# Reads of the turned queries and keys of the second attention, and its rotary steps: another place in the queue and another engine

## The chip, the cores and the metric

The kernel runs on one core of one Trainium2 chip. The metric is the device time of one execution in microseconds. Five engines work beside each other, each through its own queue of instructions in a fixed order: TensorE (PE) multiplies matrices, with its weight loads counted apart (PEld), VectorE (DVE), ScalarE (ACT) and GpSimd (POOL) work on tiles, and SyncE (SP) issues nearly all DMA transfers. An instruction waits on semaphores for what it reads or overwrites, and whatever stands behind it in its queue waits with it.

## The reference

A decoder trunk of two layers on 256 tokens of width 1024, in float32. In each layer:

```
h = rms_norm(x)
cq, ckv, k_rope, mq, mk, mv, rq, rk, rv, rg, g_mla, g_moba, g_ret = split(h @ w_in)
o_mla  = mla_branch(...)          # first attention: 8 heads, low-rank q and kv, rotary part of 32
o_moba = moba_branch(mq, mk, mv)  # second attention: 8 heads of 64, rotary on the first 16 of 64
o_ret  = retention_branch(...)    # 4 heads, rotary on all 64, chunks of 128, group norm
x = x + (sigmoid(g_mla) * (o_mla @ w_mla) + sigmoid(g_moba) * (o_moba @ w_moba)
         + sigmoid(g_ret) * (o_ret @ w_ret)) @ w_out
x = x + square(relu(rms_norm(x) @ w_up)) @ w_down
```

and a final rms_norm. With 256 tokens and blocks of 256 the second attention is plain causal attention within one block: softmax(q k^T / 8) v, where q and k have had `apply_rope`, [x1 c - x2 s, x1 s + x2 c], on their first 16 columns. c and s are tables of position and frequency.

## The kernel before

Every product is made of three float32r matmuls: weight and activation are split in a high and a low part, and hi*hi, hi*lo, lo*hi are summed (`three`, lines 300 to 303). Weights come in blocks of 128 x 1024 (512 KB) by SyncE's queue (`transfer`, line 213) into one of seven raw buffers; ScalarE copies the high part (line 280), VectorE subtracts for the low part (line 282), six buffers each. `load_w` fetches one block beyond the one in use in the order of the program, but the planner, which orders each engine's queue by a simulated timeline with the program's order as precedence, lets later blocks go ahead as buffers come free.

The program of a layer is a list of units, each some matmuls of one weight block: the compressed queries and keys of the first attention and mq (mixed in layer 0, unit "start"; units "b0" and "mq" in layer 1), mk (4 blocks), then qrope, mv 0, qnope, mv 1, kvup, mv 2, mv 3, then the gates gmla0, gmla1, gmoba0, gmoba1 of four blocks each, then rqk, rv, rg, gret0, gret1, the branches, w_out and the MLP. Other work is hung on units by `at(slot(key, j), step)`: the step is traced right after that unit. The steps around the change are these.

- `qrope` (layer line 951) leaves in `qr` the rotary columns of the first attention's queries; `swapped` (line 509) moves them, with halves exchanged, through four DMAs of SyncE into `qkoth`. `qr_rope`, at mv 0, multiplies both by tables (line 969) and adds them into the tile Q (lines 972 and 973; four adds, of which head h needs one).
- The first attention's scores (`ps_s`, line 995) of heads 0 to 3 stand at mv 3, so ahead of the gates, and those of heads 4 to 7 seven units later. The softmax is on VectorE and ScalarE (lines 556 to 574), the turned probabilities go out and back through DRAM (lines 611 and 619).
- `exchange` takes the projected mq or mk, scales the two row tiles on ScalarE (line 881), turns 32 x 32 blocks on VectorE (line 331), and calls `exchanged`: one write of 512 KB to a DRAM tile `bounce` (line 478), and eight reads of 128 KB from it (line 483), four into a tile in head order and four into a tile with the partner halves (mqraw and mqoth, mkraw and mkoth). It does so for retention's rqk as well.
- `rope_turned` makes one half of the heads: raw times cos, partner times sin (line 499), and the sum of both (line 500) in a tile qkT. For mq and mk, through `moba_rope`, the three run on GpSimd; for retention's rqk on VectorE. In layer 1 moba_rope stands at mv 0, mv 2, gmla0 1 and gmla0 3, in layer 0 at gmla1 1, gmla1 2, gmoba0 0 and gmoba0 1. The tables TAB are loaded once (line 983), traced behind the unit mv 3 of layer 0, which has fetched the block gmla0 0.
- The second attention's scores (line 543) read qkT at gmoba1 1 and, for heads 4 to 7, eight units later.

`tc.keep_in_program_order(i)` puts the instruction i behind the one traced just before it in its engine's queue. It ties i to nothing else: others may pass between, and it doesn't wait for anything to finish.

Of the kernel before, what the change touches and what calls it, by code (L numbers as in the profile page):

```python
# [7 lines left out]
F32 = mybir.dt.float32  # L8
# [6 lines left out]
P = 128  # L15
D = 1024
S = 256
# [134 lines left out]
def trunk(ctx: ExitStack, tc: tile.TileContext, gx, wts, consts, gfin, gn, xtok, out):  # L152


    nc = tc.nc
# [6 lines left out]
    dr = ctx.enter_context(tc.tile_pool(name="dr", bufs=1, space=bass.MemoryType.DRAM))  # L162
# [9 lines left out]
    TAB = cp.tile([P, 2 * S], F32, name="TAB")  # L172
# [23 lines left out]
    behind = {}  # L196
# [97 lines left out]
    def w2k(name):  # L294
        return sb.tile([P, 512], F32, name=name, tag="w2k", bufs=W2K)
# [12 lines left out]
    def halves(tile_):  # L308
        return tile_.rearrange("p (two s) -> p two s", two=2)
# [17 lines left out]
    def blocks_tile(name):  # L327
        return sb.tile([P, 4 * S], F32, name=name + "blocks", tag="probT", bufs=2)

    def turn_row(blocks, t, row):  # L330
        return nc.vector.transpose(blocks.rearrange("p (b j t e) -> p t j b e", b=4, j=4, t=2)[:, t], row)
# [137 lines left out]
                i = turn * count + j  # L469
                prog.append(((key, i), lambda i=i, ts=ts, j=j: unit(i, ts, j)))  # L470

    def exchanged(rows, name, tags):

        blocks = blocks_tile(name)
        for t in range(NT):
            turn_row(blocks, t, rows[t])
        bounce = dr.tile([P, 4 * S], F32, name="bounce", bufs=2)
        nc.sync.dma_start(bounce, blocks)
        both = [wp.tile([P, 4 * S], F32, name=name + part, tag=tag, bufs=1) for part, tag in zip(("raw", "oth"), tags)]
        for flip, dst in enumerate(both):  # L480
            for b in range(4):
                src = bounce.rearrange("(a p) (b r) -> b p a r", a=4, b=4)[b ^ flip]
                nc.sync.dma_start(dst[32 * b : 32 * b + 32, :].rearrange("p (a r) -> p a r", a=4), src)  # L483
        return both

    def rope_turned(both, tab, i, engine, pins=((), ())):

        o = sb.tile([P, 2 * S], F32, name="qkT", bufs=4)
        wide = o.rearrange("p (j t a e) -> p j t a e", j=2, t=NT, a=4)
        raw, other = (w.rearrange("p (a j t e) -> p j t a e", a=4, j=4, t=NT)[:, 2 * i : 2 * i + 2] for w in both)  # L490
        cos, sin = (
            tab[:, S * k : S * k + S].rearrange("p (t a e) -> p t a e", t=NT, a=4)[:, None].to_broadcast([P, 2, NT, 4, 32])
            for k in range(2)
        )
        for on, dst, src, by, after in ((engine, wide, raw, cos, pins[0]), (nc.gpsimd, other, other, sin, pins[1])):
            with ExitStack() as pinned:
                for ins in after:
                    pinned.enter_context(tc.issue_after(ins.ins))
                (engine if engine is nc.vector else on).tensor_mul(dst, src, by)
        engine.tensor_add(wide, wide, other)  # L500
        return halves(o)

    def swapped(raw, late=False):
# [259 lines left out]
    def at(slot, step):  # L763
        steps.setdefault(slot, []).append(step)

    def slot(key, j):
        return [k for k, _ in prog].index((key, j))
# [9 lines left out]
    def layer(l, xn, before):  # L777

        c0 = []
        c, mla, mqkv, rqkv = {}, {}, {}, {}  # L780
# [91 lines left out]
        qkT = {"mq": {}, "mk": {}}  # L872

        def moba_rope(key, i):
            qkT[key][i] = rope_turned(mqkv[key], TAB, i, nc.gpsimd)

        def exchange(key, accs):

            rows = [w2k("rows") for _ in range(NT)]
            for t in range(NT):  # L880
                nc.scalar.activation(rows[t], accs[t], AF.Copy, scale=xn.col[t])
            mqkv[key] = exchanged(rows, key, ("tsums", "thi") if key == "mk" else ("tlo", "exch"))

        if l:
            project(l, "mq", xn, 512, lambda accs: exchange("mq", accs))
            for n in range(KD):
                at(slot("b0", 7), lambda n=n: xn.square(n))
            at(slot("b0", 7), c_copies)
            at(slot("mq", 0), c_squares)
            at(slot("mq", 1), c_norms)  # L890
        else:
            mq = []
            for k in range(KD):
                prog.append((("start", k), lambda k=k: start(k, mq)))
            at(slot("start", KD - 2), lambda: xn.stats_rows(xrows))
            at(slot("start", KD - 1), c_copies)
            at(slot("start", KD - 1), c_squares)
            at(slot("start", KD - 1), c_norms)
            at(slot("start", KD - 1), lambda: exchange("mq", mq))
        project(l, "mk", xn, 512, lambda accs: exchange("mk", accs))  # L900


# [78 lines left out]
        th_mla = gates(l, "gmla", xn)  # L981
        if l == 0:
            at(slot("mv", 3), lambda: tc.keep_in_program_order(nc.sync.dma_start(TAB, consts[:, K_TURNED_MB:])))
        for i in range(2):
            if l:
                at(slot("mv", 2 * i), lambda i=i: moba_rope("mq", i))
                at(slot("gmla0", 1 + 2 * i), lambda i=i: moba_rope("mk", i))
        first = slot("mv", 3)
        at(first, lambda: omlaT.extend((t4("omlah"), t4("omlal"))))

# [25 lines left out]
            tc.keep_in_program_order(nc.sync.dma_start(rqkv["dec"][:, cs], consts[:, K_DEC:K_TURNED_RT]))  # L1016

        merged, mT = {}, []
        if l == 0:

            for i, (key, j) in enumerate((("gmla1", 1), ("gmla1", 2), ("gmoba0", 0), ("gmoba0", 1))):
                at(slot(key, j), lambda i=i: moba_rope(("mk", "mq")[i % 2], i // 2))
        first = slot("gmoba1", 1)
        at(first, lambda: omobaT.extend((t4("omobah"), t4("omobal"))))

# [24 lines left out]
        def ret_exchange(accs):  # L1050
            rows = [w2k("rows") for _ in range(NT)]
            for t in range(NT):
                nc.scalar.activation(rows[t], accs[t], AF.Copy, scale=xn.col[t])
            rqkv["both"] = exchanged(rows, "rqk", ("tsums", "thi"))

        def ret_rope(i):
            tab = rqkv["dec"][:, RT_H * 3 * P :]
            rT.append(rope_turned(rqkv["both"], tab, i, nc.vector, ((), behind["po"][1:] if i else ())))

        rT, or_ps, aT, rg, oret, oret_T = [], [], {}, {}, [], []  # L1060

# [67 lines left out]
        def oret_split():  # L1129
            oretT.extend((t4("oreth"), t4("oretl")))  # L1130
            have(4)
            with tc.issue_after(fetched[-1].ins):
                split_turned(oret_T[0], oretT)

        project(l, "rqk", xn, 512, ret_exchange)
        project(l, "rv", xn, 512, ret_done("rv"))
        for i in range(2):
            at(slot("rv", 2 + i), lambda i=i: ret_rope(i))
# [401 lines left out]
        for t in range(NT):  # L1540
            y = sb.tile([P, D], F32, name="y", tag="t4", bufs=T4)
            r = sb.tile([P, 1], F32, name="fr", tag="st", bufs=SMALL)
# [34 lines left out]
    for l in range(L):  # L1577
        xn, before = layer(l, xn, before)
# [97 lines left out]
```

## Time and profile before

| | |
|---|---|
| Median of 3 runs | 813.29 us (813.04 to 814.06) |
| Profiled execution | 813.15 us, span 811.4 us |
| Granted TensorE clock, mean | 0.995 |
| ScalarE busy | 488.6 us, 744 instructions |
| HBM traffic | 243 GB/s over the span |

The span is the time from the first to the last instruction of the profiled execution; its own time has 1.75 us more around it. "Busy" is the time in which an engine worked on some instruction. A matmul's row shows 0.39 us from issue to end, though one is issued every 0.23 us: they overlap, and their starts are what counts. In a row of waits, the wait is put down to the instruction whose semaphore came last. In a timeline, like instructions in a row are merged (x4), and the second column runs from the first one's start to the last one's end.

### The profile page before, as it was taken

The numbers are of one execution on the slowest core, as the hardware profiler recorded it, in microseconds if no ns is written. First come the engines' busy times: TensorE is split into PE (matmuls) and PEld (weight loads), VectorE is DVE, ScalarE is ACT, GpSimd is POOL, SyncE is SP. The second block draws the span as 40 slices with busy tenths as digits, with TensorE's granted clock in tenths as the row PEclk, the third lists the DMA queues.
The fourth block names the chain that finished last, engine by engine and source line by source line (L and its number), as shares of the span: only waits on it lengthen the run. The fifth ranks groups of instructions, "written<-read, shape, count | busy, mean of one in ns | idle before, by whom it ended". The sixth has DMA issues, their size and how long they took to land.

```text
span 811.4 us, 11168 instructions
## 1 busy us (share of the span) xinstructions
PE 798.2 (98%) x3815; PEld 660.4 (81%) x3815; DVE 663.8 (82%) x1112; ACT 488.6 (60%) x744; POOL 72.0 (9%) x61
## 2 busy tenths in 40 slices
PE   9998999999999999999999999999999999999997
PEld 7886887778888888888898788877888888888885
DVE  6749975988797888888797796679798888899785
ACT  7782755454476566666486756654535666667572
POOL 0136000010030000000014700001000300000000
PEclk9998999999999999999999999999999999999999
DMA  9995997787666777778739759687846677688851
GB/s 333 397 248 182 283 293 249 182 299 226 233 211 215 246 263 260 257 245 255 243 126 298 244 216 323 220 226 242 298 157 246 225 237 284 213 302 301 271 181 53
DMA packets 73880, 198.38 MB, mean 245 GB/s; under 512 B 8416, under 2 KB 31072, under 8 KB 73824
## 3 DMA queue, kind: packets, MB, share of 16 engines
q1 hardware_dynamic: 73248, 196.81, 73.9%
q10 hardware_dynamic: 576, 0.87, 0.3%
q8 instruction: 30, 0.49, 0.2%
q14 instruction: 26, 0.21, 0.1%
HBM read 175.10 MB, written 22.02 MB: 243 GB/s over the span
## 4 chain that ended last, share of the span: by engine, by line
PE 81%; DMA 7%; DVE 5%; ACT 2%; SPq 2%; issue 1%; POOL 0%; DVEq 0%; ACTq 0%
PE acc L301 16%; PE acc L303 15%; PE acc L302 15%; PE pup L301 8%; PE pup L302 8%; PE pup L303 8%; PE acc L1233 6%; DMA raw<-wts 3%; DVE wlo L282 2%; PE ps_s L995 2%; DMA bounce<-rqkblocks 1%; SPq L483 1%; ACT whi L280 1%; DMA rqkoth<-bounce 1%; DMA xrow<-xtok 1%
## 5 line engine op out<-in xcount | busy, mean ns | idle before, releaser
L282 DVE TENSOR_TENSOR wlo<-raw,whi 128x1024 fp32r<-128x1024 f32 (+3 forms) x263 | 311.7, 1202 | 68.8 <-ACT whi L280 66.9
L280 ACT ACTIVATE whi<-raw 128x1024 fp32r<-128x1024 f32 (+3 forms) x263 | 264.4, 1019 | 170.6 <-PE acc L303 95.5
L301 PE MATMUL acc<-whi,xs 128*128 128x512 f32 (+1 forms) x384 | 150.2, 393 | 0.8 <-ACT th L675 0.8
L302 PE MATMUL acc<-wlo,xs 128*128 128x512 f32 (+1 forms) x384 | 150.3, 392 | 0.0
L303 PE MATMUL acc<-whi,xs 128*128 128x512 f32 (+1 forms) x384 | 149.0, 389 | 0.0
L302 PE MATMUL pup<-wlo,xs 128*128 128x512 f32 x256 | 99.8, 390 | 0.0
L303 PE MATMUL pup<-whi,xs 128*128 128x512 f32 x256 | 99.6, 389 | 0.0
L301 PE MATMUL pup<-whi,xs 128*128 128x512 f32 x256 | 99.4, 389 | 0.0
L301 PEld LDWEIGHTS acc<-whi,xs 128*128 128x128 f32 x384 | 72.2, 188 | 16.7 <-ACT th L675 1.3
L303 PEld LDWEIGHTS acc<-whi,xs 128*128 128x128 f32 x384 | 72.3, 188 | 14.4
L302 PEld LDWEIGHTS acc<-wlo,xs 128*128 128x128 f32 x384 | 72.4, 189 | 14.2
L303 PE MATMUL acc<-whi,sq 128*128 128x512 f32 x184 | 71.8, 390 | 0.0
L301 PE MATMUL acc<-whi,sq 128*128 128x512 f32 x184 | 71.8, 390 | 0.0
L302 PE MATMUL acc<-wlo,sq 128*128 128x512 f32 x184 | 71.6, 389 | 0.0
L303 PEld LDWEIGHTS pup<-whi,xs 128*128 128x128 f32 x256 | 48.1, 188 | 10.0
L302 PEld LDWEIGHTS pup<-wlo,xs 128*128 128x128 f32 x256 | 48.1, 188 | 9.8
L301 PEld LDWEIGHTS pup<-whi,xs 128*128 128x128 f32 x256 | 47.9, 188 | 9.7
L565 ACT ACTIVATE prob<-prob,smx 128x128 f32<-128x128 f32 x64 | 28.3, 444 | 42.0 <-DVE smx L562 42.0
L392 POOL TENSOR_TENSOR sqsum<-sqsum,xsq 128x256 f32<-128x256 f32 x16 | 18.3, 1141 | 303.1 <-ACT xs L317 164.8
L303 PEld LDWEIGHTS acc<-whi,sq 128*128 128x128 f32 x184 | 34.5, 188 | 7.8 <-DVE sq L322 0.6
L301 PEld LDWEIGHTS acc<-whi,sq 128*128 128x128 f32 x184 | 34.6, 188 | 7.0
L302 PEld LDWEIGHTS acc<-wlo,sq 128*128 128x128 f32 x184 | 34.5, 188 | 7.1
(274 smaller groups left out, 1265.8 us busy)
## 6 DMA issues: line engine op xcount, KB each, us to landing
raw<-wts SPq DMA_DIRECT2D x264, 512.0 KB, 5.1
bounce<-hblocks SPq DMA_DIRECT2D x16, 512.0 KB, 3.7
hturned<-bounce SPq DMA_DIRECT2D x64, 128.0 KB, 3.1
pbounce<-blocks SPq DMA_DIRECT2D x8, 768.0 KB, 6.2
probT<-pbounce SPq DMA_DIRECT2D x32, 192.0 KB, 5.4
raw<-wts SPq DMA_DIRECT2D x5, 464.0 KB, 6.0
raw<-wts SPq DMA_DIRECT2D x4, 416.0 KB, 4.1
dec<-consts SPq DMA_DIRECT2D x2, 768.0 KB, 8.9
```

The lines of the kernel that those rows point to most:

```text
L280: fetched.append(nc.scalar.activation(hi[:, cs], raw[:, cs], AF.Copy))
L282: nc.vector.tensor_sub(lo[:, cs], raw[:, cs], hi[:, cs].bitcast(F32))
L301: nc.tensor.matmul(o, ah, bh, start=start, stop=False, **more)
L302: nc.tensor.matmul(o, ah, bl, start=False, stop=False, **more)
L303: nc.tensor.matmul(o, al, bh, start=False, stop=stop, **more)
L392: (nc.gpsimd if n < self.on_pool else nc.vector).tensor_add(self.sum, self.sum, sq)
L483: nc.sync.dma_start(dst[32 * b : 32 * b + 32, :].rearrange("p (a r) -> p a r", a=4), src)
L565: nc.scalar.activation(p[:, a:b], p[:, a:b], AF.Exp, bias=m[:, 2 + i : 3 + i], scale=d**-0.5, accum_out=m[:, 4 + i : 5 + i])
L995: nc.tensor.matmul(bank[:, o], mla["Q"][:, h, qs], mla["K"][:, h, ks], start=True, stop=True)
L1233: nc.tensor.matmul(o, a, b, start=half == 0 and i == 0, stop=4 * half + n == KD and i == len(jobs) - 1)
```

## The change

The eight reads of `exchanged` become a function of their own, `partners`, and for mq and mk they are traced at the units gmla0 0 and gmla0 2, each pinned behind the one traced before it on SyncE's queue. The DRAM tile of the write-out gets a name of its own with four slots. `rope_turned` loses its engine: all its steps run on VectorE. `moba_rope` stands at gmla1 1, gmla1 2, gmoba0 1 and gmoba0 3 in both layers, in the order mk, mq, mk, mq. For retention the reads still follow the write at once.

```diff
-    def exchanged(rows, name, tags):
+    def exchanged(rows, name):
 
         blocks = blocks_tile(name)
         for t in range(NT):
             turn_row(blocks, t, rows[t])
-        bounce = dr.tile([P, 4 * S], F32, name="bounce", bufs=2)
+        bounce = dr.tile([P, 4 * S], F32, name="rowsbounce", bufs=4)
         nc.sync.dma_start(bounce, blocks)
+        return bounce
+
+    def partners(bounce, name, tags):
+
         both = [wp.tile([P, 4 * S], F32, name=name + part, tag=tag, bufs=1) for part, tag in zip(("raw", "oth"), tags)]
         for flip, dst in enumerate(both):
             for b in range(4):
                 src = bounce.rearrange("(a p) (b r) -> b p a r", a=4, b=4)[b ^ flip]
-                nc.sync.dma_start(dst[32 * b : 32 * b + 32, :].rearrange("p (a r) -> p a r", a=4), src)
+                dma = nc.sync.dma_start(dst[32 * b : 32 * b + 32, :].rearrange("p (a r) -> p a r", a=4), src)
+                if name != "rqk":
+                    tc.keep_in_program_order(dma)
         return both
 
-    def rope_turned(both, tab, i, engine, pins=((), ())):
+    def rope_turned(both, tab, i, pins=((), ())):
...
-        for on, dst, src, by, after in ((engine, wide, raw, cos, pins[0]), (nc.gpsimd, other, other, sin, pins[1])):
+        for dst, src, by, after in ((wide, raw, cos, pins[0]), (other, other, sin, pins[1])):
             with ExitStack() as pinned:
                 for ins in after:
                     pinned.enter_context(tc.issue_after(ins.ins))
-                (engine if engine is nc.vector else on).tensor_mul(dst, src, by)
-        engine.tensor_add(wide, wide, other)
+                nc.vector.tensor_mul(dst, src, by)
+        nc.vector.tensor_add(wide, wide, other)
         return halves(o)
...
         def moba_rope(key, i):
-            qkT[key][i] = rope_turned(mqkv[key], TAB, i, nc.gpsimd)
+            qkT[key][i] = rope_turned(mqkv[key], TAB, i)
...
-            mqkv[key] = exchanged(rows, key, ("tsums", "thi") if key == "mk" else ("tlo", "exch"))
+            mqkv[key] = exchanged(rows, key)
+
+        def fetch_partners(key):
+            mqkv[key] = partners(mqkv[key], key, ("tsums", "thi") if key == "mk" else ("tlo", "exch"))
...
-        for i in range(2):
-            if l:
-                at(slot("mv", 2 * i), lambda i=i: moba_rope("mq", i))
-                at(slot("gmla0", 1 + 2 * i), lambda i=i: moba_rope("mk", i))
+        for i, key in enumerate(("mq", "mk")):
+            at(slot("gmla0", 2 * i), lambda key=key: fetch_partners(key))
...
-        if l == 0:
-
-            for i, (key, j) in enumerate((("gmla1", 1), ("gmla1", 2), ("gmoba0", 0), ("gmoba0", 1))):
-                at(slot(key, j), lambda i=i: moba_rope(("mk", "mq")[i % 2], i // 2))
+        for i, (key, j) in enumerate((("gmla1", 1), ("gmla1", 2), ("gmoba0", 1), ("gmoba0", 3))):
+            at(slot(key, j), lambda i=i: moba_rope(("mk", "mq")[i % 2], i // 2))
...
-            rqkv["both"] = exchanged(rows, "rqk", ("tsums", "thi"))
+            rqkv["both"] = partners(exchanged(rows, "rqk"), "rqk", ("tsums", "thi"))
 
         def ret_rope(i):
             tab = rqkv["dec"][:, RT_H * 3 * P :]
-            rT.append(rope_turned(rqkv["both"], tab, i, nc.vector, ((), behind["po"][1:] if i else ())))
+            rT.append(rope_turned(rqkv["both"], tab, i, ((), behind["po"][1:] if i else ())))
```

## Rows read from the trace of the kernel before

**Rows 1.** The page, its first lines: the span, and the busy time of each engine with its share of the span and its count of instructions.

```profile
span 811.4 us, 11168 instructions
...
PE 798.2 (98%) x3815; PEld 660.4 (81%) x3815; DVE 663.8 (82%) x1112; ACT 488.6 (60%) x744; POOL 72.0 (9%) x61
```

**Rows 2.** TensorE's waits over the whole span: who waited for whom, us in total, times, longest.

```profile
PE ps_s L995 <- DVE Q L972: 3.7, 2, 2.7
PE por L1080 <- DVE retA L1072: 0.9, 2, 0.6
...
PE ps_s L995 <- DVE Q L973: 0.8, 1, 0.8
```

**Rows 3.** Timeline of TensorE around the first attention's first scores in layer 0: start, us, instruction, in brackets the idle time before it and what ended it.

```profile
62.55 0.39 PE L301 MATMUL acc<-whi,xs 128*128 128x512 f32 x1
65.59 0.89 PE L995 MATMUL ps_s<-KK,Q 128*128 128x128 f32 x4 [2.66 <-DVE Q L972]
...
73.30 0.40 PE L302 MATMUL acc<-wlo,xs 128*128 128x512 f32 x1
```

**Rows 4.** The same view for layer 1: first the same place, then around its second score group (heads 4 to 7).

```profile
462.55 0.39 PE L303 MATMUL acc<-whi,xs 128*128 128x512 f32 x1
...
467.10 0.39 PE L302 MATMUL acc<-wlo,xs 128*128 128x512 f32 x1
...
482.33 0.39 PE L303 MATMUL acc<-whi,xs 128*128 128x512 f32 x1
...
485.41 0.40 PE L302 MATMUL acc<-wlo,xs 128*128 128x512 f32 x1
...
485.87 0.39 PE L301 MATMUL acc<-whi,xs 128*128 128x512 f32 x1
```

**Rows 5.** Busy time of each engine in a stretch of layer 0: the stretch, its length, busy time of PE, PEld, DVE, ACT, POOL (with counts), then granted clock, DMA share, GB/s.

```profile
66.00:72.20 6.20, 5.31 (x16) 3.38 (x15) 6.11 (x4) 0.00 (x0) 6.20 (x5) 0.54 0.09 38
```

**Rows 6.** Timeline of ScalarE in layer 0: the copy that makes qr.

```profile
47.20 0.59 ACT L951 COPY qr<-pqr 128x512 f32<-128x512 f32 x1
```

**Rows 7.** Timeline of SyncE's queue in layer 0: start, us of issuing, what is issued.

```profile
30.43 0.42 SPq L983 DMA_DIRECT2D TAB<-consts  x1
32.56 0.33 SPq L213 DMA_DIRECT2D raw<-wts  x1
...
34.96 4.44 SPq L213 DMA_DIRECT2D raw<-wts  x3
40.29 0.33 SPq L478 DMA_DIRECT2D bounce<-mkblocks  x1
...
50.01 4.63 SPq L483 DMA_DIRECT2D mkoth<-bounce  x4
55.14 2.49 SPq L509 DMA_DIRECT2D qkoth<-qr  x4
```

**Rows 8.** Timeline of VectorE in layer 0, the rotary steps of Q and the weight splits about them.

```profile
59.14 0.69 DVE L969 TENSOR_TENSOR qr<-qr,K 128x512 f32<-128x512 f32 x1 [2.28 <-DMA qkoth<-qr]
59.75 1.79 DVE L969 TENSOR_TENSOR qkoth<-qkoth,K 128x512 f32<-128x512 f32 x1
61.46 2.32 DVE L282 TENSOR_TENSOR wlo<-raw,whi 128x1024 fp32r<-128x1024 f32 x1
...
70.49 5.54 DVE L282 TENSOR_TENSOR wlo<-raw,whi 128x1024 fp32r<-128x1024 f32 x3
```

**Rows 9.** The instructions on the tile Q between 55 and 75 us: ns shortest, median and longest, and the start of the first and the last.

```profile
L972 DVE TENSOR_TENSOR Q<-qr,qkoth x2: 1636/1640/1645, 63.8 to 67.1; 64x512 f32<-64x512 f32 x2
L973 DVE TENSOR_TENSOR Q<-qr,qkoth x2: 1636/1638/1640, 65.5 to 68.8; 64x512 f32<-64x512 f32 x2
```

**Rows 10.** Timeline of VectorE in layer 1, the same steps.

```profile
456.98 1.24 DVE L969 TENSOR_TENSOR qr<-qr,K 128x512 f32<-128x512 f32 x1 [2.97 <-DMA qkoth<-qr]
...
462.18 1.66 DVE L972 TENSOR_TENSOR Q<-qr,qkoth 64x512 f32<-64x512 f32 x1
...
464.59 0.69 DVE L972 TENSOR_TENSOR Q<-qr,qkoth 64x512 f32<-64x512 f32 x1
```

**Rows 11.** Timeline of GpSimd: its last rotary steps in layer 0 and in layer 1.

```profile
69.88 3.93 POOL L500 TENSOR_TENSOR qkT<-qkT,mkoth 128x512 f32<-128x512 f32 x2
...
459.32 3.97 POOL L500 TENSOR_TENSOR qkT<-qkT,mkoth 128x512 f32<-128x512 f32 x2
```

**Rows 12.** Groups of instructions over the span, shapes kept apart: count, busy us, mean ns of one, idle time before. First GpSimd's adds for mk, then VectorE's steps for retention, then its splits of whole weight blocks between 76 and 106 us, when GpSimd is idle.

```profile
L500 POOL TENSOR_TENSOR qkT<-qkT,mkoth 128x512 f32<-128x512 f32 x4 | 7.9, 1994 | 0.0
...
L499 DVE TENSOR_TENSOR qkT<-rqkraw,dec 128x512 f32<-128x512 f32 x4 | 2.6, 688 | 4.6 <-DMA rqkraw<-bounce 4.6
...
L500 DVE TENSOR_TENSOR qkT<-qkT,rqkoth 128x512 f32<-128x512 f32 x4 | 2.7, 682 | 0.0
...
L282 DVE TENSOR_TENSOR wlo<-raw,whi 128x1024 fp32r<-128x1024 f32 x12 | 14.2, 1219 | 2.7 <-ACT whi L280 2.6
```

**Rows 13.** Busy time of each engine from the end of the mk projection to the second attention's scores, layer 0 and layer 1; columns as in rows 5.

```profile
44.00:106.00 62.00, 58.46 (x272) 47.86 (x272) 48.74 (x98) 38.23 (x73) 20.38 (x12) 0.94 0.82 244
444.00:505.00 61.00, 59.95 (x298) 50.10 (x298) 48.52 (x99) 40.32 (x74) 16.80 (x10) 1.00 0.81 263
```

**Rows 14.** DMA issues between 47.8 and 57.7 us: count, KB each, median us from issue to landing.

```profile
mkoth<-bounce SPq DMA_DIRECT2D x4, 128.0 KB, 6.6
qkoth<-qr SPq DMA_DIRECT2D x4, 64.0 KB, 2.6
```

## The prediction

> **What bounds the kernel now.** I read the page first, then TensorE's own waits, then the stretches where it waits, engine by engine. TensorE is busy 798.2 us of 811.4 [rows 1], so most work on other engines can grow or shrink without being seen; what counts is where TensorE stands still or runs below its clock. Its list of waits names one place above all [rows 2]: the scores of the first attention (ps_s, line 995) wait for Q, which VectorE finishes, 3.7 us at line 972 and 0.8 us at line 973. Retention's values wait 0.9 us for VectorE, in two pieces; nothing else in the body reaches 1 us.
>
> The list understates it. In layer 0 the last matmul of the value projection starts at 62.55 and the fourth matmul of the gates behind the scores at 73.30, 10.75 us later [rows 3]. The undisturbed case is the second score group of layer 1: from 482.33 to the fourth matmul behind it at 485.87 is 3.54 us, to the second at 485.41 it is 3.08 us [rows 4]. So layer 0 loses 10.75 - 3.54 = 7.21 us. Layer 1 goes from 462.55 to the second matmul at 467.10, 4.55 us [rows 4], a loss of 4.55 - 3.08 = 1.47 us. Together 8.68 us. In layer 0 a part of this is clock: from 66.0 to 72.2 us TensorE was granted 0.54 [rows 5].
>
> Why Q is late: two causes. First, the move of Q's partner halves (qkoth, line 509) sits in SyncE's queue behind the sixteen reads of line 483; the copy qr is done at 47.20 + 0.59 = 47.79 [rows 6], its move is issued only at 55.14, right after the four mkoth reads took SyncE from 50.01 to 54.64 [rows 7]. VectorE idles 2.28 us for it and begins at 59.14 [rows 8]. Second, VectorE is then slow. All four adds into Q take 1.64 us in layer 0 [rows 9]; in layer 1 the first takes 1.66 us, the third 0.69 [rows 10]. What differs is GpSimd: it runs the moba rotary steps until 73.81 in layer 0 (69.88 + 3.93) and until 463.29 in layer 1 [rows 11], and the layer-1 adds drop to 0.69 us right after 463.29. The multiply of qkoth (1.79 us against 0.69 for its twin) and the weight splits (2.32 and three in 5.54 us) in rows 8 show the same.
>
> **The change part by part.**
>
> *Rotary steps from GpSimd to VectorE.* Removed: 24 GpSimd instructions, about 2 us each (1994 ns) [rows 12], which nobody on the way to the end waits for. Added: 24 VectorE instructions of the same shape; retention's own steps price them at 0.688 us for a multiply and 0.682 for the add [rows 12], so 24 x 0.685 = 16.4 us, 8.2 us a layer. Given back in layer 0: four adds x (1.64 - 0.69) = 3.8, the multiply 1.1, one split 2.32 - 1.2 = 1.1 (the mean of the undisturbed group is 1.2 [rows 12]), three splits 5.54 - 3.5 = 2.0; in all 8.0 us. From 44 to 106 us VectorE is busy 48.74 of 62 us [rows 13]; afterwards 48.74 - 8.0 + 8.2 = 48.9 us in 62 - 7.2 = 54.8 us. In layer 1 it is busy 48.52 of 61 us [rows 13]; even with nothing given back, 48.52 + 8.2 = 56.7 fits 61 - 1.5 = 59.5. I cost the steps at 0 on the path: this idle time covers them, and their reader, the second attention's scores, comes at the end of the stretch. If the cover failed, the six steps of the first four heads, 6 x 0.685 = 4.1 us, would stand before those scores in each layer: bounds 0 and 8.2 us in all. I take 0, nearest to rows 13. A gain beyond the one counted under Q's rope is excluded: in the rest of the stretch no row shows TensorE waiting for VectorE.
>
> *Q's rope.* With GpSimd quiet and the queue order unchanged, VectorE starts at 59.14 and needs two multiplies (1.4), one split (1.2) and four adds at about 0.72: the last ends near 64.6. The scores could begin one matmul step of 0.23 us (half of 485.41 to 485.87 [rows 4]) after 62.55, at 62.78; the group takes 3.08 less two steps, 2.6 us, so its last head, a quarter, wants Q at 62.78 + 0.75 x 2.6 = 64.75. So the 7.21 us go even then. In layer 1 the same sum from its own start is earlier still (first add at 462.18 with the slow steps in front of it [rows 10]), so the 1.47 us go too.
>
> *Reads traced later.* Sixteen read DMAs of 128 KB a layer are the same in number and size; only their place changes. A pin (keep_in_program_order) holds an instruction behind the one traced before it on its queue, and no more: the table load TAB is pinned behind the block for the first gate and yet was issued at 30.43 us [rows 7], some 30 us ahead of the gate it is traced next to. The mq reads are now held behind the second gate block, the mk reads behind the fourth; in layer 0, after TAB, one block was issued at 32.56 and three between 34.96 and 39.40, so the first gate's four were out before the mk write at 40.29 [rows 7]. So the pins hardly bind there; what changes is precedence, since qkoth and its rope are now traced ahead of the reads. If qkoth goes first, it leaves at about 47.8, takes 2.49 us to issue and 2.6 us to land [rows 7, 14], and Q is done by about 52.9 + 1.4 + 1.2 + 2.9 = 58.4, 4 us early. Cost on the path between 0 (either order above) and rival 1's 2.8 us; I take 0, since Q's steps are traced ahead of the moba steps on VectorE as well; below 0 there is nothing left to gain once Q is early. Queued behind a rotary step that waits for a read would be weight splits; they run up to six buffers ahead of TensorE, so a wait of 2 us there costs nothing. Write-outs and rqk's reads keep their size; the separate four-slot bounce could only take away a wait for a slot, and no row shows one: 0.
>
> *Sum.* 813.15 us (profiled execution, span 811.4 plus 1.75 around it) - 7.21 - 1.47 = 804.5. Something as small as rows 2's other waits, 0.7 us, I expect to appear in their stead: 805.2. The median shown, 813.29, is 0.14 above the profiled one, within its own spread.
>
> **Rivals.**
>
> *1. The reads don't leave the way.* Precedence decides nothing if mk's reads are ready first, and VectorE then takes the mk steps before Q. All reads had landed by 59.14. Four steps left (2.7), two multiplies (1.4), a split (1.2): the adds end at 65.1 to 67.3, 2.5 us too late; in layer 1, where its idle time ends at 456.98 [rows 10], the same steps end 2.16 us earlier against the scores' start, 0.3 us too late. That is 804.5 + 2.8 = 807.3, and with half a microsecond of low clock 807.8. For it: SyncE's order in rows 7. Against: the traced order.
> The row on the clock says that a 2.66 us gap with stuttering behind it brought 0.54 [rows 3, 5]. The Trainium skill, "TensorE: Matmul & The Clock Gate", Part 1, "What's actually happening", has the clock halved only after an idle window of about 3.4 us; by it 2.5 us of wait would cost nothing more, 807.3; by the row perhaps 3 us at half clock, 1.5 us more, 808.8. No single gap here is 3.4 us, so the trace doesn't bear the rule out to the letter.
>
> *2. VectorE becomes the bound.* If the softmax chain leaves the steps no room and the first six stand before the second attention's scores in both layers: 804.5 + 8.2 = 812.7, no change that can be told. For it: VectorE's 48.74 of 62 us lie unevenly. Against: the sums above.
>
> *3. Slower.* VectorE works in order. If a moba step is queued ahead of Q and its read lands later than now, because the reads start later, everything behind it stands, Q first. With d us of later landing, rival 1's losses become 2.5 + d and 0.3 + d; 8.68 is used up at d = 2.9 us. At d = 5 (the mkoth reads take 6.6 us to land in layer 0 [rows 14]) the time is 804.5 + 2.8 + 10 = 817.3. Against: Q would have to be overtaken by work traced later, in both layers.
>
> **How the numbers follow.** Forecast 0.64, rival 1 0.18, rival 2 0.10, rival 3 0.08. The first two lie below 811.66, more than 0.2% faster, which is about what a measurement of this kernel tells from no change; of rival 2 I put 0.03 there too: faster 0.85, within 0.2% 0.07, slower 0.08. The range 803.6 to 810.0 starts at the full 8.68 us with 0.9 us (retention's waits) on top, holds forecast, rival 1 and part of rival 2.
>
> **What would show it.** Right: no wait of ps_s for Q in the list of TensorE; about 3 us between the last value matmul and the gates in both layers; clock 1.0 there; adds into Q at 0.69 us; GpSimd at 72.0 - (20.38 + 16.80) = 35 us or less [rows 1, 13]; VectorE's total nearly as before. Wrong: a wait of ps_s on Q or, at the second attention (line 543), on qkT; VectorE idle on mkraw, mkoth or mqoth ahead of Q; SyncE still issuing line 483 before line 509 with Q late.

## The result and the profile after

The changed kernel takes 805.07 us (median of four runs, 803.88 to 805.70) against 813.16 us before (812.49 to 814.06): a ratio of 0.9898, interval 0.9881 to 0.9915, about 8.1 us. The profiled execution took 804.96 us with a span of 803.2. The forecast was 805.2.

The first lines of the page, to be set beside [rows 1]: span, instructions, busy time of each engine with its count.

```profile
span 803.2 us, 11159 instructions
PE 794.2 (99%) x3815; PEld 659.0 (82%) x3815; DVE 662.0 (82%) x1136; ACT 488.9 (61%) x744; POOL 30.3 (4%) x37
```

VectorE does 24 instructions more in no more time (1136 in 662.0 us against 1112 in 663.8): what it took over from GpSimd it got back by running undisturbed. GpSimd falls from 72.0 to 30.3 us.

TensorE's waits over the whole span, whole list: who waited for whom, us in total, times, longest.

```profile
PE por L1085 <- DVE retA L1077: 0.9, 2, 0.6
PE acc L301 <- ACT th L681: 0.8, 2, 0.4
PE warm L763 <- PEq L1674: 0.8, 1, 0.8
```

The two rows of scores waiting for Q [rows 2], three waits in all, are gone. What is left was there before and is small. Next, busy time by stretch (the stretch, its length, busy time of PE, PEld, DVE, ACT, POOL, then granted clock, DMA share, GB/s); the first and the last answer to [rows 13], the middle one is the stretch of [rows 5].

```profile
44.00:98.80 54.80, 54.80 (x272) 45.96 (x270) 46.54 (x110) 37.99 (x71) 0.00 (x0) 1.00 0.85 254
66.00:72.20 6.20, 6.20 (x33) 4.91 (x31) 6.07 (x9) 2.29 (x4) 0.00 (x0) 1.00 0.52 159
436.00:496.00 60.00, 60.00 (x298) 50.77 (x298) 51.07 (x114) 40.61 (x75) 0.00 (x0) 1.00 0.83 271
```

TensorE is busy without a break at full clock in both layers, where it had 58.46 of 62 us and a clock of 0.54 in the worst 6.2. Layer 0 makes its 272 matmuls in 7.2 us less.

So far this is the forecast. The place where Q is made looks different from it, though. VectorE in layer 0 (start, us from first start to last end, instruction, idle time before it), to be set beside [rows 8, 9]:

```profile
51.33 1.29 DVE L505 TENSOR_TENSOR mqoth<-mqoth,TAB 128x512 f32<-128x512 f32 x2 [3.09 <-issue]
...
56.91 0.69 DVE L505 TENSOR_TENSOR qkT<-mkraw,TAB 128x512 f32<-128x512 f32 x1 [3.15 <-DMA mkraw<-rowsbounce]
...
59.32 0.68 DVE L978 TENSOR_TENSOR qr<-qr,K 128x512 f32<-128x512 f32 x1
59.93 0.69 DVE L978 TENSOR_TENSOR qkoth<-qkoth,K 128x512 f32<-128x512 f32 x1
60.53 0.68 DVE L506 TENSOR_TENSOR qkT<-qkT,mqoth 128x512 f32<-128x512 f32 x1
...
62.27 1.28 DVE L505 TENSOR_TENSOR mkoth<-mkoth,TAB 128x512 f32<-128x512 f32 x2
...
65.32 0.69 DVE L981 TENSOR_TENSOR Q<-qr,qkoth 64x512 f32<-64x512 f32 x1
...
67.47 0.69 DVE L982 TENSOR_TENSOR Q<-qr,qkoth 64x512 f32<-64x512 f32 x1
```

The lengths are right: 0.69 us for each add into Q, and the multiply of qkoth back from 1.79. The order isn't. VectorE takes ten steps of the second attention before the first add into Q: two multiplies on mqoth at 51.33, and eight from 56.91 on (two on mkraw, two on mqraw, two on mkoth, two sums for mq). That add begins at 65.32, in the kernel before at 63.81: Q is later at its start and 2.3 us earlier at its end (68.16 against 68.82 + 1.64 = 70.46). And TensorE, beside [rows 3]:

```profile
65.98 0.39 PE L301 MATMUL acc<-whi,xs 128*128 128x512 f32 x1
66.20 2.93 PE L1002 MATMUL ps_s<-KK,Q 128*128 128x128 f32 x16
68.79 0.58 PE L302 MATMUL acc<-wlo,xs 128*128 128x512 f32 x1
```

It comes to the scores at 66.20, 0.19 us after the first add has ended (66.01), and not at 62.8. In the order of the trace 312 matmuls stand ahead of the scores; before the change there were 297. In layer 1 it is the other way about: 2187 against 2190. The order of each queue is made ahead of the run, so a second thing had changed that the forecast had not reckoned with. This is what the experiments are about.

SyncE's queue in layer 0 (start, us of issuing, what):

```profile
40.33 3.13 SPq L487 DMA_DIRECT2D mqraw<-rowsbounce  x4
...
48.19 1.85 SPq L487 DMA_DIRECT2D mkraw<-rowsbounce  x4
50.32 0.30 SPq L487 DMA_DIRECT2D mkoth<-rowsbounce  x1
51.24 4.93 SPq L515 DMA_DIRECT2D qkoth<-qr  x4
56.23 1.54 SPq L487 DMA_DIRECT2D mkoth<-rowsbounce  x3
```

The move into qkoth begins 3.9 us earlier than in [rows 7], but it takes 4.93 us to issue, not 2.49, and the mq reads and five of the mk reads still go ahead of it. VectorE starts on qr no earlier than before (59.32 against 59.14).

### The profile page after: what moved, and what is told of

Read it like the earlier page. It is cut to its first block, busy times and chain, and to the rows that moved or that the text cites. A ratio compares the mean times of both kernels' runs of the same rounds, so it can differ in the third digit from the quotient of the medians.

```text
span 803.2 us, 11159 instructions
## 1 busy us (share of the span) xinstructions
PE 794.2 (99%) x3815; PEld 659.0 (82%) x3815; DVE 662.0 (82%) x1136; ACT 488.9 (61%) x744; POOL 30.3 (4%) x37
## 4 chain that ended last, share of the span: by engine, by line
PE 91%; DVE 3%; DMA 3%; ACT 1%; issue 1%; SPq 1%; DVEq 0%
PE acc L301 17%; PE acc L303 17%; PE acc L302 17%; PE pup L302 8%; PE pup L301 8%; PE pup L303 8%; PE acc L1238 6%; PE acc L855 1%; DVE wlo L282 1%; PE ps_s L1002 1%; DMA rowsbounce<-rqkblocks 1%; DMA rqkoth<-rowsbounce 1%; SPq L487 1%; ACT whi L280 1%; DMA raw<-wts 0%
## 5 line engine op out<-in xcount | busy, mean ns | idle before, releaser
L282 DVE TENSOR_TENSOR wlo<-raw,whi 128x1024 fp32r<-128x1024 f32 (+3 forms) x263 | 304.7, 1174 | 56.8 <-ACT whi L280 54.7
L1238 PE MATMUL acc<-mT,whi 128*128 128x512 f32 (+1 forms) x144 | 35.2, 371 | 0.0
```

The costliest lines, as they stand in the source:

```text
L282: nc.vector.tensor_sub(lo[:, cs], raw[:, cs], hi[:, cs].bitcast(F32))
L1238: nc.tensor.matmul(o, a, b, start=half == 0 and i == 0, stop=4 * half + n == KD and i == len(jobs) - 1)
```

## The experiments

Three theories stood at the start: the engine alone makes the gain (no GpSimd step beside VectorE); the later reads make it; it takes the two together. All kernels keep the whole computation; two have extra work on GpSimd that nobody reads.

### One half of the change at a time

The kernel before with nothing but the engine of the second attention's steps changed:

```diff
-            qkT[key][i] = rope_turned(mqkv[key], TAB, i, nc.gpsimd)
+            qkT[key][i] = rope_turned(mqkv[key], TAB, i, nc.vector)
```

> The kernel before with one edit: moba's rotary steps on VectorE; reads and slots stay. Theory G (GpSimd beside VectorE made Q late, the reads' place does not matter): 804.5 to 806.5 us, adds into Q at 0.69 us, no wait of the scores for Q. Rival R (the reads ahead of qkoth in SyncE's queue made Q late): 811 to 813 us, since the reads still stand there. Rival O (TensorE's planned order, gate matmuls ahead of the scores, hides a late Q): about 805 too, with Q's last add in layer 0 ending after 65 us and the scores starting later than 62.8.

Measured: 805.73 us (804.87 to 807.29), ratio 0.9903 [0.9886, 0.9920].

The changed kernel with its steps back on GpSimd, the reads as changed:

```diff
-            qkT[key][i] = rope_turned(mqkv[key], TAB, i)
+            qkT[key][i] = rope_turned(mqkv[key], TAB, i, engine=nc.gpsimd)
```

> The changed kernel with moba's rotary steps back on GpSimd; reads and slots as changed. G: 811 to 814 us, adds into Q at about 1.6 us again, TensorE waiting for Q in layer 0 for 2 us or more. R: 805 to 807 us. O: as G, since here the planner puts the scores even a few matmuls further ahead than before.

Measured: 814.54 us (813.11 to 817.08), ratio 1.0008 [0.9996, 1.0019]. Its list of TensorE's waits begins:

```profile
PE ps_s L1002 <- DVE Q L981: 4.7, 2, 3.9
PE ps_s L1002 <- DVE Q L982: 1.9, 3, 0.8
```

The changed kernel with the reads behind the write again, and the changed kernel with the reads in their new place but without the pins:

```diff
             mqkv[key] = exchanged(rows, key)
+            fetch_partners(key)
...
-            at(slot("gmla0", 2 * i), lambda key=key: fetch_partners(key))
```

> The changed kernel with the reads of mq and mk traced right behind their write again, without pins; rotary steps on VectorE at the changed slots. G: 804.5 to 806.5 us. R: 811 to 813 us. O: about 805, with gate matmuls ahead of the scores.

```diff
-                if name != "rqk":
-                    tc.keep_in_program_order(dma)
```

> The changed kernel without the pins on the reads of mq and mk. The planned queues differ from the changed kernel's in one place alone, one weight block and one mqraw read swapped in layer 1. All theories: 804 to 806 us, no difference. Only if a pin held back a transfer that matters would it move by more than 1 us.

Measured: 804.78 us (804.00 to 806.62), ratio 0.9894 [0.9878, 0.9909], and 804.61 us (803.66 to 806.21), ratio 0.9890 [0.9875, 0.9905].

What follows: the engine alone brings the gain, 0.9903 against 0.9898 with intervals that cover each other. The place of the reads and the pins are worth nothing that can be told, in either company. With the engine alone the signs named for rival O came too: Q's last add in layer 0 ends only at 69.73 and the scores start at 70.48. The time cannot tell that rival from G; the next experiments take up the order.

### What makes Q early enough: its start, or the order of TensorE

The changed kernel with the second attention's steps held behind Q's last add on VectorE (the pins of rope_turned, on mla["last"]):

```diff
-                nc.vector.tensor_add(mla["Q"][0:64, 2 * b + 1 :: 4, :], qr[rows], qo[rows])
+                mla["last"] = nc.vector.tensor_add(mla["Q"][0:64, 2 * b + 1 :: 4, :], qr[rows], qo[rows])
...
-            qkT[key][i] = rope_turned(mqkv[key], TAB, i)
+            qkT[key][i] = rope_turned(mqkv[key], TAB, i, ([mla["last"]], [mla["last"]]))
```

> The changed kernel with moba's rotary steps queued behind Q's last add on VectorE; TensorE's order left to the planner. O: TensorE does not wait in the changed kernel, so nothing is left to gain: 804.5 to 806 us. Rival W (the late Q still costs something that the list of waits does not show): 803 to 804 us.

Measured: 804.50 us (803.61 to 806.11), ratio 0.9898 [0.9884, 0.9913]. Q is done at 62.79 instead of 68.16, and nothing is gained: an early Q was not needed.

The changed kernel with all matmuls of the block gmla0 held behind the first scores on TensorE, and the same with the steps held behind Q as well:

```diff
+            with ExitStack() as pinned:
+                if key == "gmla0":
+                    pinned.enter_context(tc.issue_after(scored[-1].ins))
                 for kk in range(per):
...
-                    nc.tensor.matmul(bank[:, o], mla["Q"][:, h, qs], mla["K"][:, h, ks], start=True, stop=True)
+                    scored.append(nc.tensor.matmul(bank[:, o], mla["Q"][:, h, qs], mla["K"][:, h, ks], start=True, stop=True))
```

> The changed kernel, with the matmuls of the first gate queued behind the first attention's scores on TensorE in both layers, as they stood before; nothing else edited. O (the planner's new order hides a late Q in layer 0): the first add into Q ends near 66.0 us, the scores could start at 62.8, so 3 to 5 us of wait come back there: 808 to 811 us. Rival E (Q is early enough by itself, the order is beside the point): 804.5 to 806 us, no wait for Q.

> As x5_scores_first, and moba's rotary steps are queued behind Q's last add on VectorE. O: Q's last add ends before 64.7 us, the wait goes again: 804.5 to 806 us. Rival L (Q is late because qkoth lands late, whatever stands ahead of it on VectorE): as x5_scores_first, 808 to 811 us.

Measured: 818.49 us (817.89 to 819.25), ratio 1.0069 [1.0054, 1.0084], and 812.88 us (809.13 to 816.50), ratio 0.9996 [0.9977, 1.0014]. TensorE in the first of them, layer 0:

```profile
54.68 0.39 PE L303 MATMUL acc<-whi,xs 128*128 128x512 f32 x1
65.96 0.55 PE L1007 MATMUL ps_s<-KK,Q 128*128 128x128 f32 x1 [10.89 <-DVE Q L986]
```

And VectorE in the second, layer 0, where Q's steps come first:

```profile
58.51 0.69 DVE L983 TENSOR_TENSOR qr<-qr,K 128x512 f32<-128x512 f32 x1 [7.51 <-DMA qkoth<-qr]
```

Both times lie above every range given for them. The first expectation took the gates to have stood behind the scores before the change; 34 of their matmuls stood ahead, so this order is tighter than the old one, and TensorE is at the scores at 55.07 (54.68 + 0.39), not at 62.8. Without gate matmuls to put in front, it stands 10.89 us for Q. Taking the second attention's steps out of Q's way saves 5.6 us of time (818.49 - 812.88); 8.4 us remain to 804.50. There TensorE still waits 6.0 us for Q, and Q's steps start late because VectorE idles 7.51 us for qkoth, as rival L had it. What the steps cost here is rival 1's mechanism, and its price is large where nothing covers it.

Two more experiments at the same place. First, the changed kernel with only the first 33 matmuls of gmla0 in layer 0 free to pass the scores (34 stood there before the change, 49 after; counted as matmuls beyond the 263 that stand ahead in the kernel with the gates behind the scores):

```diff
+                        if l == 0 and key == "gmla0":
+                            ahead.append(1)
+                            if len(ahead) > 11:
+                                pinned.enter_context(tc.issue_after(scored[-1].ins))
                         three(accs[t][:, :n], ah[:, sl], al[:, sl], wh[:, kk, :], wl[:, kk, :], k == 0, k == KD - 1)
```

> The changed kernel, but in layer 0 only 33 gate matmuls may stand ahead of the first attention's scores on TensorE, about as many as in the kernel before (the changed kernel has 49 there). All steps stay on VectorE. If the gain of layer 0 comes from the two things together, rotary steps at their undisturbed length and more gate matmuls in front of the scores, TensorE reaches the scores near 62.6 us while VectorE, which takes the second attention's steps first, adds into Q from 65.3 to 68.2 us: the list of waits shows about 3 us of scores on Q, with 1 us more of low clock, and the time is 808 to 810 us. If the freed VectorE alone brings the gain, Q is early enough also for this order: 804.5 to 805.5 us.

Measured: 806.15 us (804.86 to 806.58), ratio 0.9898 [0.9884, 0.9912]. The edit missed its aim: 310 matmuls stand ahead of the scores in this kernel's trace, so the planner filled the forbidden places with others, and the scores start at 66.96 without a wait. It says nothing on the price of the old place.

Second, the kernel of the 812.88 us with the mk reads queued behind the move into qkoth:

```diff
+                    if name == "mk":
+                        pinned.enter_context(tc.issue_after(moved[-1].ins))
-                if name != "rqk":
-                    tc.keep_in_program_order(dma)
```

> The kernel with all gate matmuls behind the scores and Q's steps ahead of the second attention's (812.9 us when it ran), with one thing more: the eight mk reads are queued behind the move into qkoth on SyncE. If the late move is a cause of its own, qkoth lands near 53 us instead of 58, Q's adds run from about 55.5 to 58.4 us, TensorE, which comes to the scores near 55.2 us, waits 1 to 2.5 us, and the time is 805.5 to 808.5 us. If the move is not what makes Q late in that kernel, the time stays at 812 to 814 us.

Measured: 813.00 us (809.76 to 814.66), ratio 0.9992 [0.9979, 1.0005], so no faster, and in the range given for a move that is not the cause. In its profiled execution (its fastest, 809.76 us) TensorE waits 3.9 us for Q, against 6.0 without the edit. SyncE and VectorE there:

```profile
48.85 2.48 SPq L521 DMA_DIRECT2D qkoth<-qr  x4
51.37 4.05 SPq L495 DMA_DIRECT2D mkraw<-rowsbounce  x4
```

```profile
56.34 0.69 DVE L985 TENSOR_TENSOR qr<-qr,K 128x512 f32<-128x512 f32 x1 [5.44 <-DMA qkoth<-qr]
```

The move is issued by 51.33, 4.8 us earlier than in the changed kernel, but VectorE has it only at 56.34: the median from issue to landing is 6.0 us here, against 5.0 in the changed kernel and 2.6 in [rows 14]. In this stretch of all the traces SyncE's transfers land in the order in which they were issued. Here the last weight block ahead of the move, issued at 47.58, lands at 55.10, and the four parts of the move land from 55.45 to 56.26; in the changed kernel they land from 57.75 to 58.99. So a place ahead of the eight mk reads brought the landing forward by 2.7 us and not by 4.8: the move still came in behind what had been issued before it.

### What GpSimd does to VectorE

The kernel with the steps on GpSimd and the one with the steps behind Q have the same order of TensorE's queue, matmul for matmul, with 289 ahead of the first scores. In the second Q's adds run at 0.69 us, in the first (VectorE, layer 0):

```profile
63.06 1.63 DVE L981 TENSOR_TENSOR Q<-qr,qkoth 64x512 f32<-64x512 f32 x1
64.72 1.64 DVE L982 TENSOR_TENSOR Q<-qr,qkoth 64x512 f32<-64x512 f32 x1
66.39 1.65 DVE L981 TENSOR_TENSOR Q<-qr,qkoth 64x512 f32<-64x512 f32 x1
68.08 1.65 DVE L982 TENSOR_TENSOR Q<-qr,qkoth 64x512 f32<-64x512 f32 x1
```

To hold GpSimd's part by itself, the changed kernel was given GpSimd work that nobody reads, beside the same stretch: 16 multiplies a layer from tiles in SBUF, or one multiply and 40 memsets a layer. SBUF is the memory on the chip in which the tiles stand. The queues of the other four engines are as in the changed kernel, instruction for instruction.

```diff
+        def beside():
+            scratch = sb.tile([P, 2 * S], F32, name="scratch", bufs=1)
+            low = c["l"][:, 0:2, :].rearrange("p k s -> p (k s)").bitcast(F32)
+            for _ in range(16):
+                nc.gpsimd.tensor_mul(scratch, low, low)
+
+        at(slot("mk", 3), beside)
```

> The changed kernel plus 16 multiplies a layer on GpSimd, 128x512, both inputs in SBUF, result to a tile that nothing reads, started when the compressed queries are turned (about 43 us in layer 0), so that they run beside Q's steps. The queues of the four other engines come out the same as in the changed kernel. C (a GpSimd instruction that reads SBUF blocks VectorE's instructions with two SBUF inputs): adds into Q go from 0.69 to about 1.6 us, Q's last add in layer 0 ends after 72 us, 809 to 816 us. Rival N (GpSimd was not in the way, only its results were late): adds stay at 0.69 us, 804.5 to 806 us.

> The changed kernel plus one multiply and 40 memsets a layer on GpSimd at the same place into the same unread tile: GpSimd is busy but reads nothing. C with reads alone in the way: adds into Q stay at 0.69 us, 804.5 to 806 us. Rival A (any GpSimd work on SBUF slows VectorE): adds into Q slower while the memsets run, 807 us or more.

Measured: 818.97 us (818.05 to 819.85), ratio 1.0066 [1.0050, 1.0082], with the multiplies; 804.40 us (803.39 to 806.38), ratio 0.9892 [0.9869, 0.9914], with the memsets. The same VectorE step, first beside the multiplies, then beside the memsets:

```profile
61.61 1.52 DVE L986 TENSOR_TENSOR qr<-qr,K 128x512 f32<-128x512 f32 x1
63.06 1.52 DVE L986 TENSOR_TENSOR qkoth<-qkoth,K 128x512 f32<-128x512 f32 x1
```

```profile
59.50 0.68 DVE L987 TENSOR_TENSOR qr<-qr,K 128x512 f32<-128x512 f32 x1
60.10 0.69 DVE L987 TENSOR_TENSOR qkoth<-qkoth,K 128x512 f32<-128x512 f32 x1
```

GpSimd was busy in both (groups over the span; count, busy us, mean ns):

```profile
L939 POOL TENSOR_TENSOR scratch<-cTl 128x512 f32<-128x512 f32 x32 | 46.4, 1451 | 19.0 <-DVE cTl L318 16.7
```

```profile
L940 POOL MEMSET scratch<- 128x512 f32 x80 | 42.1, 526 | 4.6
```

So 46.4 us of GpSimd that reads costs 13.9 us of time (818.97 against 805.07), most of it in two waits: 4.0 us for a weight split in layer 0 and 5.0 us for Q in layer 1, with low clock behind each (0.72 from 66 to 72 us, 0.63 from 466 to 472). The time is above the range of C, and one sign of C did not come: the adds into Q stay at 0.69 us, as in rival N. The multiplies end at 66.93 (42.59 + 24.34), before the first add at 70.98; it is the steps ahead of the adds that are longer, and so Q's last add ends only at 73.82. 42.1 us that only writes costs nothing. The Trainium skill, "SBUF — State Buffer", "Who interferes with whom", says that a VectorE instruction with two inputs in SBUF contends with a GpSimd instruction that reads SBUF, not with one that only writes it. These two runs agree: 1.52 against 0.68 us. They do not prove it by themselves, since a multiply and a memset differ in more than in reading.

Last, a version meant to have both: the steps on GpSimd, but none before Q's last add (a small GpSimd add that reads Q, and the steps held behind it).

```diff
+            if "after" not in mla:
+                mla["after"] = nc.gpsimd.tensor_add(small("tick")[0:64, 0:2], mla["Q"][0:64, 7, 0:2], mla["Q"][0:64, 3, 0:2])
-            qkT[key][i] = rope_turned(mqkv[key], TAB, i, engine=nc.gpsimd)
+            qkT[key][i] = rope_turned(mqkv[key], TAB, i, ([mla["after"]], [mla["after"]]), nc.gpsimd)
```

> The changed kernel with moba's rotary steps on GpSimd, but held behind Q's last add by a small GpSimd add that reads Q. G as it stands (GpSimd beside VectorE costs only where TensorE waits for VectorE): VectorE is slowed by some 5 to 8 us a layer in the gates, where no one waits: 804.5 to 807 us. Rival V (VectorE has no room in the gates): 808 to 813 us, with waits of the gates for weight splits or of the second attention's scores for qkT.

Measured: 822.49 us (820.98 to 823.07), ratio 1.0115 [1.0100, 1.0130], the slowest of all and above both ranges. Q was in time, with adds of 0.69 us and no wait for it. The four other queues are those of the kernel with the steps on GpSimd, instruction for instruction. What came instead is rival V's sign, larger than it was priced: TensorE waits 12.9 us for weight splits, in three waits. In VectorE's, GpSimd's and TensorE's timelines and in the view of the split's tile between 62.9 and 79.05 us (ns shortest, median, longest), it looks like this:

```profile
61.88 18.32 DVE L282 TENSOR_TENSOR wlo<-raw,whi 128x1024 fp32r<-128x1024 f32 x3
```

```profile
61.93 1.23 POOL L882 TENSOR_TENSOR tick<-Q 64x2 f32<-64x2 f32 x1 [26.64 <-DVE Q L984]
63.12 1.27 POOL L505 TENSOR_TENSOR qkT<-mkraw,TAB 128x512 f32<-128x512 f32 x1
...
76.73 1.25 POOL L506 TENSOR_TENSOR qkT<-qkT,mqoth 128x512 f32<-128x512 f32 x1
```

```profile
79.12 0.80 PE L302 MATMUL acc<-wlo,xs 128*128 128x512 f32 x1 [7.45 <-DVE wlo L282]
```

```profile
L282 DVE TENSOR_TENSOR wlo<-raw,whi x3: 1212/1226/16046, 61.9 to 79.0; 128x1024 fp32r<-128x1024 f32 x3
```

Two of the three splits take their usual 1.2 us. One takes 16.05 us: it starts at 63.02, while GpSimd's small add on Q is still running (61.93 + 1.23 = 63.16) and just before the first of its twelve steps (63.12), and ends at 79.07, after the last (76.73 + 1.25 = 77.98). The steps run back to back at 1.25 to 1.29 us each, undisturbed. In layer 1 the same: one split of 16.10 us.

## Why the prediction held, and which step of it did not

**The size of the loss: right.** From the 280th matmul to the 400th (counted from 0) the kernel before takes 32.50 us and the changed one 25.40, so layer 0 gains 7.1 (the sum had 7.21); from the 2100th to the 2300th 40.95 against 39.44, so layer 1 gains 1.51 (1.47). One label was wrong: the matmul at 62.55 in [rows 3] was no longer the value projection's but one of the 34 that already stood ahead of the scores. It was the last before the scores all the same, so the difference stands.

**The cause, GpSimd on VectorE: right, and shown** by the engine alone (805.73), by its reverse (814.54), and by the multiplies and the memsets. The other cause named, the move into qkoth behind sixteen reads, is borne out in part. The move does land late, but that costs nothing in the changed kernel; it shows only where the gates are kept from in front of the scores (812.88), and there a place ahead of the mk reads made nothing faster (813.00). Its size was wrong as well: the forecast's early case took the 2.6 us to landing of [rows 14], measured behind all the reads, and had the move landed at 52.9. Issued from 48.85 to 51.33, it took 6.0 us and landed at 56.26.

**The steps at 0 on VectorE: right.** It is busy 46.54 of 54.80 us in layer 0; the sum had 48.9.

**"I take 0, since Q's steps are traced ahead of the moba steps on VectorE as well": the value held, its reason fell.** Precedence decided nothing in layer 0, as rival 1 said, and VectorE took ten steps first. Q's adds end at 68.16; the forecast had them at 64.6, with 58.4 as the early case. Rival 1 had the losses that follow from that at 2.8 us. They did not come: TensorE has 15 more gate matmuls in front, some 3.4 us (15 of 0.23), and without these it would have been at the scores near 62.8, 3.2 us ahead of the first add. That is argued from the trace; the kernel that was to have the old number in front had 47 beyond the 263, and only the one with none in front shows such a wait (10.89 us). The forecast held the order of TensorE fixed; the planner made a new one. So the 0 was luck in the changed kernel: the losses it denied were covered by something it did not reckon with. With Q's steps first, as it had reasoned, the time is 804.50, the same. With GpSimd quiet, Q's lateness as such is worth nothing over a wide range (first add in layer 0, first scores, matmuls in front beyond 263):

| kernel | first add ends | scores start | in front | time |
|---|---|---|---|---|
| steps behind Q | 60.64 | 61.23 | 26 | 804.50 |
| without pins | 64.66 | 66.57 | 49 | 804.61 |
| changed kernel | 66.01 | 66.20 | 49 | 805.07 |
| engine alone | 67.57 | 70.48 | 65 | 805.73 |
| reads at once | 68.52 | 69.56 | 65 | 804.78 |
| steps on GpSimd | 64.69 | 64.84 (3.9 us waited) | 26 | 814.54 |
| before | 65.45 | 65.59 (2.7 us waited) | 34 | 813.16 |

In the first five the scores follow the first add by 0.2 to 2.9 us and nothing waits. In the last two TensorE comes 2.7 to 3.9 us too early, to an add that GpSimd has made 1 us longer, as it did the steps before it. Against undisturbed lengths, the steps from qr to the first add are 3.2 us longer in the kernel before and 3.8 us in the one with the steps on GpSimd, about as much as TensorE waits. So what was lost before came from VectorE falling behind an order that fits its undisturbed pace. That the planner reckons with undisturbed durations is argued from this table; no run here shows it.

**The pins "hardly bind": right.** Without them 804.61.

**Rival 2, VectorE as the bound: did not come.** No wait of the second attention's scores on qkT is in the list.

**Rival 3, slower: did not come.** VectorE does stand on a read ahead of Q, 3.15 us for mkraw until 56.91, but that read is issued at 48.19, ahead of the move, and VectorE is past it before it turns to qr at 59.32. The late ones, three mkoth reads issued until 57.77, have landed when VectorE comes to them at 62.27: no idle time stands in that row.

**What was to show it.** The signs for the forecast all came: no wait on Q, 2.81 us from the last matmul ahead of the scores to the first behind them (65.98 to 68.79; 2.66 in layer 1), clock 1.00, adds of 0.69 us, GpSimd under 35 us, VectorE's total as before. But two of the signs against it came as well: VectorE idle on mkraw ahead of Q, and most reads issued ahead of the move. They were read off VectorE and SyncE alone; they would have been signs of a loss only with TensorE already at the scores.

**The 0.7 us of something small: near in size, by luck.** No other wait of [rows 2] grew. The matmuls end 8.66 us earlier (the 3800th at 793.24 against 801.90) and the span is 8.19 shorter, so 0.47 us comes back behind the 3800th matmul. From there to the end the traces take either 9.47 or 9.93 us, give or take 0.02: 9.47 in all five kernels in which GpSimd has 61 instructions or more, 9.93 in all nine in which it has 37. So it goes with the work taken off GpSimd; why, no run here shows.

## What to carry to other kernels

A step moved to an idle engine is not free if that engine then reads SBUF beside an engine for which others wait: read the mean duration of the same instruction with and without the neighbour (0.69 against 1.64 us here) before counting idle time as room. Where a planner writes the queues, ask whether an operand is late by the plan or against it: here Q could come 8 us later (first add at 60.64 or at 68.52) at no cost as long as work stood in front, while an add about 3 us late against the planned order made TensorE wait. So look for durations that differ from their undisturbed twins, and don't hold the order of the waiting engine fixed in a forecast.

## What was not expected of the hardware

A single VectorE split of 1.22 us stood 16.05 us (16.10 in layer 1) while GpSimd ran twelve reading instructions back to back. In the kernel with the steps on GpSimd but not held back, the two engines take turns: 1.64 us for VectorE's add, and two GpSimd steps in 3.94 us (the longer one 2.27) instead of 1.25 each. In the long case GpSimd loses nothing and VectorE gets no turn between instructions. The section of the Trainium skill named above says, of VectorE's 2-port modes, that whoever issues first has the ports that it shares with GpSimd "for the whole instruction" and blocks the other; a tensor_tensor like this split has no such mode by that section, so the sentence does not settle this case. By the trace GpSimd's small add was running when the split started, so GpSimd was first; that it then kept VectorE out for twelve instructions more, the sentence does not say. What decides between taking turns and standing, no run here shows.
